# First pair of experts: gate and up weights in units of 512 KB instead of 1 MB

## The chip, the cores and the metric

The kernel runs on one core of a Trainium2 chip. The metric is the device time of one execution in microseconds (us). Before the change three runs took 1047.30, 1050.07 and 1051.92 us, with a median of 1050.07 us. The core's engines are TensorE (PE, with its weight loads PEld), VectorE (DVE), ScalarE (ACT), GpSimd (POOL) and SyncE (SP); transfers run on 16 DMA engines, and nearly all are issued by SP.

## What is computed

The reference is one layer of a decoder: 256 tokens of width 2048, four kinds of attention side by side, an output projection, and then a mixture of experts, which is where the change lies. A router gives each token two of 16 experts, and each expert is a gated network with 512 hidden columns:

```python
for e in range(N_EXPERTS):                                   # 16
    he = jax.nn.silu(t @ w_gate[e]) * (t @ w_up[e])          # (256, 2048) @ (2048, 512)
    y = y + combine[:, e:e + 1] * (he @ w_down[e])           # (256, 512) @ (512, 2048)
```

All is float32. An expert's gate, up and down weights are 4 MB each, so that the 16 experts have 192 MB of weights (MB is 1024 KB throughout). Each is read from memory once.

## The kernel before

**Stages.** The adaLN vectors, the input projection with the attention, and the output projection come first (to about 540 us); then the router, and then eight pairs of experts, `for p in range(NP)` at L1427 ff. (the lines named here are those of the profile). Up to 64 tokens an expert are gathered into slots. A pair's two experts stand side by side on TensorE: expert e = 1 on the upper 64 output partitions (L202), e = 0 on the lower (L205), so that one step is two matmuls of 512 columns.

**One pair.** The contraction of gate and up over 2048 runs in four blocks c of 512, and in each block in four steps i of 128. `GUORDER` sets the order of blocks and of gate (g = 0) and up (g = 1): gate and up of c = 0, gate and up of c = 1, gate of c = 2 and 3, up of c = 2 and 3. Then come silu and product (`sg`, `he`), four transposes (`hpT`), and the down projection `dn` in four blocks n of 512 output columns, each over four steps f of 128. A block's result is scaled (`yo`), split (`yhl`) and scattered back to the tokens by matmuls `sco`, one block later. In the first pair the gather of the tokens (`pg`, `xg`) and the gate vector's spreading (`ada_r`) run between the steps.

**The stream of weights.** `Stream` holds a list of units, in the order in which they are used, and the buffers that are free. Its `pump` takes the next unit, gives it a buffer and issues its transfer on SP; if no buffer fits, it stops, and units behind it wait too. A unit of gate or up is one block c of one expert: 128 partitions x 2048 elements, 1 MB, `(("gu", p), c, g, e)`. A unit of down is 0.5 MB, `(("dh", p, h), f, e)`: step f for half h of the output columns. Buffers are of these kinds:

- five ring buffers `r0` to `r4` of 1 MB, which are given out whole or as two halves; a unit of 1 MB needs both halves of one of them (the method `room`);
- one buffer of 0.5 MB, and several of 1 MB in other pools, which a unit of 1 MB takes whole; two units of 0.5 MB can share one, and it is given on when both are done;
- two of 1 MB that are used once and not given on (`ONCE`).

In the trace a tile takes the name of its unit (`ugu` gate or up, `udh` down, `uo` output projection) or of its ring buffer (`r`). Together they hold 13.5 MB of expert weights when the router runs.

**Order.** A scheduler orders each engine's instructions with its own estimate of times. SP's queue is worked off strictly in order: a transfer whose buffer isn't free yet holds up those behind it. Each transfer also waits for the one issued eight places earlier.

## Time and profile before

| | before |
|---|---|
| median of three runs | 1050.07 us |
| profiled execution | 1046.43 us |
| its span | 1044.7 us |
| TensorE busy | 947.1 us (91%) |
| VectorE busy | 542.3 us (52%) |
| ScalarE busy | 351.0 us (34%) |
| DMA packets moved | 371.12 MB in bytes of 10^6, mean 355 GB/s |

The profiled execution is one run of the program, 3.6 us under the median; its times are counted from the start of the span. A busy TensorE is not one at its peak, since matmuls overlap. The DMA share of a stretch says how much of it the 16 engines were moving data; the GB/s beside it what they moved. In a list of instructions, the time in brackets is the idle time of the engine before the row and what ended it.

### The profile page before, as it was taken

What the parts mean: (1) busy time and instruction counts of PE and PEld (TensorE: products, weight loads), DVE (VectorE), ACT (ScalarE), POOL (GpSimd) and SP (SyncE); (2) the same over time, 40 slices, a digit from 0 to 9 for tenths busy, and PEclk for the clock granted to TensorE, in tenths of its full rate; (3) what the DMA queues carried; (4) which work ended last, traced back from release to release, by engine and by line L of the source; (5) the groups of instructions that cost most, each with busy time, mean ns of one, the idle gap of its engine ahead of it and who ended that gap; (6) DMA issues with size and microseconds to landing.
All of it is one profiled execution on the core that took longest, in us unless ns stands there. A gap on an engine that the chain in (4) does not pass through costs nothing.

```text
span 1044.7 us, 16307 instructions
## 1 busy us (share of the span) xinstructions
PE 947.1 (91%) x6369; PEld 583.4 (56%) x6369; DVE 542.3 (52%) x1058; ACT 351.0 (34%) x759; POOL 4.3 (0%) x13
## 2 busy tenths in 40 slices
PE   5899999999999998789989998999989897999984
PEld 1677778898788986567874434323343232432323
DVE  2444466996998998879764242404033130412216
ACT  4333345566676767634453101100010000200013
POOL 0000000000000000000000000000000000000000
PEclk9999999999999999979989999999999999999997
DMA  9999999996999998799864999999999999999993
GB/s 331 357 356 360 357 326 346 347 371 213 344 329 349 343 384 319 257 331 389 303 237 159 382 419 404 420 415 416 419 412 420 412 420 413 417 417 414 420 375 108
DMA packets 149467, 371.12 MB, mean 355 GB/s; under 512 B 11485, under 2 KB 90246, under 8 KB 132746
## 3 DMA queue, kind: packets, MB, share of 16 engines
q1 hardware_dynamic: 148416, 368.41, 94.5%
q10 hardware_dynamic: 938, 1.61, 0.4%
q8 instruction: 52, 0.85, 0.3%
q14 instruction: 29, 0.24, 0.1%
q0 software_dynamic: 32, 0.01, 0.0%
HBM read 367.90 MB, written 2.10 MB: 354 GB/s over the span
## 4 chain that ended last, share of the span: by engine, by line
PE 66%; DMA 17%; DVE 10%; issue 3%; ACT 3%; SPq 0%; DVEq 0%; ACTq 0%
PE dn L202 11%; DMA r<-in_exp_w_up_dram 8%; PE acc L563 5%; PE acc L564 4%; PE acc L565 4%; PE gatep L202 4%; PE upp L202 4%; PE upp L205 3%; PE pg L1408 3%; PE oacc L567 3%; PE gatep L205 3%; PE oacc L568 3%; PE oacc L569 3%; PE ada L202 2%; DMA r<-in_w_in_dram 2%
## 5 line engine op out<-in xcount | busy, mean ns | idle before, releaser
L563 PE MATMUL acc<-Hh,wlo 128*128 128x256 f32 x512 | 145.0, 293 | 6.0 <-DVE wlo L588 3.6
L564 PE MATMUL acc<-Hl,whi 128*128 128x256 f32 x512 | 145.2, 286 | 0.0
L565 PE MATMUL acc<-Hh,whi 128*128 128x256 f32 x512 | 144.4, 285 | 0.0
L588 DVE TENSOR_TENSOR wlo<-r,whi 128x1024 fp32r<-128x1024 f32 x86 | 104.9, 1220 | 50.1 <-ACT whi L586 49.9
L586 ACT CAST whi<-r 128x1024 fp32r<-128x1024 f32 x86 | 90.0, 1048 | 85.8 <-PE acc L565 23.3
L512 DVE SCALAR_TENSOR_TENSOR ada_v<-r,cT,ada_v 128x1024 f32<-128x1024 f32 x92 | 117.7, 1279 | 0.5
L563 PEld LDWEIGHTS acc<-Hh,wlo 128*128 128x128 f32 x512 | 95.6, 191 | 16.6 <-DVE wlo L588 6.3
L1462 DVE TENSOR_TENSOR he<-upp,sg 128x128 f32<-128x128 f32 x32 | 7.1, 282 | 181.7 <-PE upp L205 181.7
L564 PEld LDWEIGHTS acc<-Hl,whi 128*128 128x128 f32 x512 | 97.8, 191 | 3.5 <-issue 2.6
L565 PEld LDWEIGHTS acc<-Hh,whi 128*128 128x128 f32 x512 | 97.7, 191 | 2.7 <-issue 2.3
L205 PE MATMUL upp<-ugu,xg 128*64 128x512 f32 x196 | 81.7, 597 | 1.3 <-DMA ugu<-in_exp_w_up_dram 1.3
L205 PE MATMUL gatep<-r,xg 128*64 128x512 f32 x192 | 80.4, 596 | 0.0
L205 PE MATMUL upp<-r,xg 128*64 128x512 f32 x172 | 72.6, 595 | 4.0 <-DMA r<-in_exp_w_up_dram 4.0
L1541 ACT CAST yhl<-yo 128x512 fp32r<-128x512 f32 x31 | 19.2, 618 | 167.5 <-DVE yo L1535 142.2
L205 PE MATMUL gatep<-ugu,xg 128*64 128x512 f32 x176 | 72.5, 602 | 0.7 <-DMA ugu<-in_exp_w_gate_dram 0.7
L1492 DVE TENSOR_TENSOR xt<-xt,sco 128x512 f32<-128x512 f32 (+1 forms) x70 | 42.0, 638 | 57.6 <-PE sco L1491 57.0
L205 PE MATMUL dn<-udh,heT 128*64 128x512 f32 x136 | 66.3, 599 | 0.0
L202 PE MATMUL dn<-udh,heT 128*64 128x512 f32 x128 | 63.3, 599 | 1.6 <-DVE heT L1479 1.6
L567 PE MATMUL oacc<-wlo,Oh 128*128 128x512 f32 (+1 forms) x160 | 59.5, 373 | 4.6 <-DVE wlo L588 2.9
L1458 ACT ACTIVATE sg<-gatep 128x512 f32<-128x512 f32 x8 | 4.8, 597 | 169.1 <-PE gatep L205 169.1
L202 PE MATMUL gatep<-ugu,xg 128*64 128x512 f32 x112 | 58.7, 610 | 1.7 <-DMA ugu<-in_exp_w_gate_dram 1.7
L202 PE MATMUL dn<-r,heT 128*64 128x512 f32 (+1 forms) x124 | 59.1, 578 | 0.5 <-DVE heT L1479 0.5
(399 smaller groups left out, 1889.3 us busy)
## 6 DMA issues: line engine op xcount, KB each, us to landing
r<-in_ada_w_dram SPq DMA_DIRECT2D x155, 512.0 KB, 7.2
ugu<-in_exp_w_gate_dram SPq DMA_DIRECT2D x36, 1024.0 KB, 13.3
r<-in_w_in_dram SPq DMA_DIRECT2D x69, 512.0 KB, 7.5
ugu<-in_exp_w_up_dram SPq DMA_DIRECT2D x34, 1024.0 KB, 14.6
udh<-in_exp_w_down_dram SPq DMA_DIRECT2D x66, 512.0 KB, 11.4
r<-in_exp_w_up_dram SPq DMA_DIRECT2D x30, 1024.0 KB, 14.1
r<-in_exp_w_down_dram SPq DMA_DIRECT2D x57, 512.0 KB, 11.4
r<-in_exp_w_gate_dram SPq DMA_DIRECT2D x28, 1024.0 KB, 13.8
```

Source lines behind the costliest of these rows:

```text
L202: ins = op(*args, **kw).ins
L205: ins = op(*args, **kw).ins
L512: V.scalar_tensor_tensor(acc, w, cT[:, u:u + 1], acc[:], OP.mult, OP.add)
L563: ins = mm(o, wl, hh, start=first, stop=False)
L564: mm(o, wh, hl, start=False, stop=False)
L565: mm(o, wh, hh, start=False, stop=last)
L567: ins = mm(o, hh, wl, start=first, stop=False)
L568: mm(o, hl, wh, start=False, stop=False)
L569: mm(o, hh, wh, start=False, stop=last)
L586: A.copy(hi, w)
L588: V.tensor_tensor(lo, w, hi[:].bitcast(F32), OP.subtract)
L1492: V.tensor_tensor(y(t, cs), y(t, cs), o, OP.add)
```

## The change

In the first pair (p = 0) a unit of gate or up is half a block, two of its four steps for one expert: 128 partitions x 1024 elements, 0.5 MB, with a key that has the half h behind it. For each block and each of gate and up there are four transfers in place of two: h = 0 of both experts, then h = 1 of both. Such a unit fits any buffer, a half of a ring buffer too. It is reported done after its two steps, instead of after all four. Units of the other seven pairs, and all down units, stay as they are, and no matmul is added or taken away.

```diff
-        us = [((("gu", p), c, g, e), mkg(c, g, e), 2) for c, g in GUORDER for e in range(2)]
+        def mkg2(c, g, e, h):
+            return lambda t: nc.sync.dma_start(t, (gateT, upT)[g][:, c, 2 * p + e, 1024 * h:1024 * h + 1024])
+
+        if p == 0:
+            us = [((("gu", p), c, g, e, h), mkg2(c, g, e, h)) for c, g in GUORDER for h in range(2) for e in range(2)]
+        else:
+            us = [((("gu", p), c, g, e), mkg(c, g, e), 2) for c, g in GUORDER for e in range(2)]
...
             keys = [(("gu", p), c, g, e) for e in range(2)]
+            half = lambda e, i: (keys[e] + (i // 2,), i % 2) if p == 0 else (keys[e], i)
...
                 for e in (1, 0):
-                    w = stream.get(keys[e])[:, 512 * i:512 * i + 512]
+                    key, at = half(e, i)
+                    w = stream.get(key)[:, 512 * at:512 * at + 512]
...
-            for key in keys:
-                stream.done(key)
+                if p == 0 and i % 2:
+                    for e in range(2):
+                        stream.done(half(e, i)[0])
+            if p:
+                for key in keys:
+                    stream.done(key)
```

The built program shows how the units stand. The number behind a tile's name is that of the buffer's allocation. SP's queue, first place: the transfers behind the last ones that find a free buffer, in pair 0's gate and up. The digits after `ugu` are p, c, g, e, and in the new kernel also h; those after `udh` are p, h, f, e. Before:

```order
L257 DMA ugu0301_6019<-in_exp_w_gate_dram 128x2048
L257 DMA ugu0310_6147<-in_exp_w_up_dram 128x2048
L257 DMA r2_96<-in_exp_w_up_dram 128x2048
L260 DMA r3_97<-in_exp_w_down_dram 128x1024
L260 DMA udh0001_6190<-in_exp_w_down_dram 128x1024 x2
L257 DMA r1_95<-in_exp_w_up_dram 128x2048
```

Now:

```order
L271 DMA ugu03011_6032<-in_exp_w_gate_dram 128x1024
L271 DMA ugu03011_6032<-in_exp_w_up_dram 128x1024
L271 DMA r0_94<-in_exp_w_up_dram 128x1024
L271 DMA r2_96<-in_exp_w_up_dram 128x1024
L271 DMA r4_98<-in_exp_w_up_dram 128x1024
L271 DMA ugu03110_6163<-in_exp_w_up_dram 128x1024
L260 DMA r1_95<-in_exp_w_down_dram 128x1024
L271 DMA r2_96<-in_exp_w_up_dram 128x1024
```

The last up units of c = 2 and 3 go, half by half, to halves of r0, r2 and r4; before, the two of c = 3 took two whole buffers, a 1 MB one and r1.

SP's queue, second place: the transfers that wait for the end of pair 0's gate and up and for its down projection. Before:

```order
L257 DMA r2_96<-in_exp_w_gate_dram 128x2048
L260 DMA udh0131_6335<-in_exp_w_down_dram 128x1024 x2
L260 DMA udh0121_6310<-in_exp_w_down_dram 128x1024 x2
L260 DMA udh0111_6307<-in_exp_w_down_dram 128x1024 x2
L257 DMA r1_95<-in_exp_w_up_dram 128x2048
L257 DMA ugu1001_6360<-in_exp_w_gate_dram 128x2048
L260 DMA udh1001_6507<-in_exp_w_down_dram 128x1024
L257 DMA ugu1011_6397<-in_exp_w_up_dram 128x2048
```

Now:

```order
L260 DMA r0_94<-in_exp_w_down_dram 128x1024
L257 DMA ugu1000_6353<-in_exp_w_gate_dram 128x2048
L260 DMA udh0130_6346<-in_exp_w_down_dram 128x1024 x2
L260 DMA udh0120_6325<-in_exp_w_down_dram 128x1024 x2
L260 DMA udh1000_6523<-in_exp_w_down_dram 128x1024
L257 DMA r2_96<-in_exp_w_gate_dram 128x2048
L257 DMA ugu1010_6412<-in_exp_w_up_dram 128x2048
L257 DMA r1_95<-in_exp_w_up_dram 128x2048
```

Before, the last transfer that waits for gate and up of pair 0 alone is `ugu1001`; now it is the one to r2, a unit of 1 MB earlier, and `ugu1010` waits for the down projection. A half of r0 and one of r4, which held up weights of c = 3, take nothing until units of 1 MB of pair 1 go to r0 and r4, behind the down projection.

TensorE, third place: the middle of pair 0's down projection, behind its first two blocks. Before:

```order
L1386 MATMUL sp_6535<-ident_80,oh4_6074 128x128 x2
L202 MATMUL dn_6417<-r0_94,heT_6373 64x512
L205 MATMUL dn_6417<-r4_98,heT_6373 64x512
L202 MATMUL dn_6417<-udh0111_6307,heT_6373 64x512
L205 MATMUL dn_6417<-r0_94,heT_6373 64x512
```

Now:

```order
L1392 MATMUL sp_6553<-ident_80,oh4_6089 128x128 x2
L202 MATMUL gatep_6489<-r2_96,xg_6100 64x512
L205 MATMUL gatep_6489<-ugu1000_6353,xg_6100 64x512
...
L202 MATMUL dn_6432<-r3_97,heT_6388 64x512
L205 MATMUL dn_6432<-udh0031_6256,heT_6388 64x512
L202 MATMUL dn_6432<-r0_94,heT_6388 64x512
L205 MATMUL dn_6432<-r4_98,heT_6388 64x512
```

Pair 1's gate of c = 0 (eight matmuls) has moved ahead of blocks n = 2 and 3 of the down projection; before, it stands behind both.

## Rows read from the trace of the kernel before

**Rows 1.** The page: span, then DMA share and GB/s in 40 slices

```profile
span 1044.7 us, 16307 instructions
...
DMA  9999999996999998799864999999999999999993
GB/s 331 357 356 360 357 326 346 347 371 213 344 329 349 343 384 319 257 331 389 303 237 159 382 419 404 420 415 416 419 412 420 412 420 413 417 417 414 420 375 108
```

**Rows 2.** Chain of waits in order of time: start us, us, what

```profile
685.66 15.01 DMA r<-in_exp_w_up_dram
...
982.19 16.70 DMA r<-in_exp_w_up_dram
```

**Rows 3.** Windows of 10 us: engines' busy time and count, PEclk, DMA share, GB/s

```profile
540.00:550.00 10.00, 5.79 (x29) 4.90 (x30) 8.21 (x36) 9.87 (x18) 0.00 (x0) 0.60 0.50 198
550.00:560.00 10.00, 10.00 (x48) 4.43 (x46) 5.72 (x12) 5.12 (x9) 0.00 (x0) 0.89 0.00 0
560.00:570.00 10.00, 10.00 (x54) 4.33 (x50) 3.65 (x7) 1.13 (x2) 0.00 (x0) 1.00 0.72 267
570.00:580.00 10.00, 10.00 (x58) 5.21 (x56) 3.22 (x7) 1.49 (x3) 0.00 (x0) 1.00 0.98 374
580.00:590.00 10.00, 10.00 (x50) 3.49 (x46) 1.60 (x6) 2.67 (x4) 0.00 (x0) 1.00 0.90 338
590.00:600.00 10.00, 9.48 (x51) 4.20 (x50) 2.01 (x7) 0.59 (x1) 0.00 (x0) 1.00 1.00 404
600.00:610.00 10.00, 10.00 (x46) 3.27 (x42) 5.41 (x10) 1.85 (x3) 0.00 (x0) 1.00 1.01 419
640.00:650.00 10.00, 7.52 (x48) 4.78 (x44) 3.42 (x9) 2.43 (x5) 0.00 (x0) 1.00 1.04 403
660.00:670.00 10.00, 10.00 (x46) 3.43 (x44) 5.84 (x9) 1.85 (x3) 0.00 (x0) 1.00 1.02 419
```

**Rows 4.** Timeline of SP, its issues: start us, us, engine, line, operation

```profile
541.31 0.33 SPq L257 DMA_DIRECT2D ugu<-in_exp_w_gate_dram  x1
560.57 0.33 SPq L257 DMA_DIRECT2D ugu<-in_exp_w_up_dram  x1
560.99 0.38 SPq L257 DMA_DIRECT2D r<-in_exp_w_up_dram  x1
...
591.89 0.33 SPq L257 DMA_DIRECT2D r<-in_exp_w_up_dram  x1
592.31 0.38 SPq L257 DMA_DIRECT2D ugu<-in_exp_w_gate_dram  x1
```

**Rows 5.** Timeline of TensorE in pair 0 and at pair 1's start

```profile
555.58 0.59 PE L205 MATMUL upp<-r,xg 128*64 128x512 f32 x1
...
559.95 0.59 PE L205 MATMUL upp<-r,xg 128*64 128x512 f32 x1
...
594.18 0.64 PE L202 MATMUL dn<-udh,heT 128*64 128x512 f32 x1 [0.52 <-DVE heT L1479]
...
601.57 0.64 PE L202 MATMUL dn<-r,heT 128*64 128x512 f32 x1
...
605.15 0.72 PE L1490 MATMUL sco<-yhl,M 128*128 128x512 f32 x2
...
606.28 0.64 PE L202 MATMUL dn<-r,heT 128*64 128x512 f32 x1
...
610.18 0.64 PE L202 MATMUL gatep<-ugu,xg 128*64 128x512 f32 x1
...
613.76 0.50 PE L1490 MATMUL sco<-yhl,M 128*128 128x512 f32 x1
```

**Rows 6.** Windows of 2 us, columns as in rows 3

```profile
560.00:562.00 2.00, 2.00 (x14) 1.20 (x12) 0.28 (x1) 0.00 (x0) 0.00 (x0) 1.00 0.33 49
562.00:564.00 2.00, 2.00 (x12) 0.57 (x8) 1.45 (x3) 0.56 (x1) 0.00 (x0) 1.00 0.82 336
```

**Rows 7.** The page, part 6: a group of issues, us to landing

```profile
udh<-in_exp_w_down_dram SPq DMA_DIRECT2D x66, 512.0 KB, 11.4
```

## The prediction

> **What bounds the kernel now.** I read the page's slices first. The 16 DMA engines are busy nine tenths or more from about 575 us to the end, at 404 to 420 GB/s, after a dip at 520 to 575 us [rows 1]. So from there on the kernel runs at the pace of the weight stream. The chain of waits says the same: six times TensorE ends a pair of experts waiting 15 to 20 us for an up weight, first at 685.66 us, last at 982.19 us [rows 2]. What follows the last of these is TensorE's and VectorE's tail. The end therefore moves by as much as the stream moves, and the stream's place is fixed by the last moment at which the queue had nothing to do. In the windows of 10 us that is the dip: 198 GB/s, then 0, then 267, 374, 338, then 404 and 419 [rows 3]. TensorE is busy nearly all of these windows but the first, so it isn't TensorE that waits there. SyncE's own rows tell why the stream stops: between the issues at 541.31 and 560.57 us lie 19 us, and it then goes on with two units of 1 MB [rows 4]. All buffers are full, and the first to come free are those of the up weights of c = 0, when TensorE has read both units whole, at 560.5 us [rows 5]; the gate units of c = 0 sit in the two buffers that are used once and free nothing.
>
> **A ledger of the stream.** I count in MB of 1024 KB; 419 GB/s is 0.40 MB/us. When the stream stops, 13.5 MB of expert weights have landed (13 units of 1 MB and a down unit). With the windows of [rows 3] the kernel before has moved 16.05 MB by 570 us, 19.6 by 580, 22.85 by 590, 26.7 by 600, 30.7 by 610, and so 31.5 MB at 612.0 us. From then on it doesn't stop.
>
> **What the change adds and moves.** Sixteen units of 1 MB become 32 of 0.5 MB: the same bytes, 16 more issues of 0.33 us on SyncE [rows 4], which waits for buffers anyway: nothing. No matmul is added. Eight transfers can be in flight (each also waits for the one eight places ahead), which with halves is 4 MB or 10 us of the stream: it doesn't run dry for that, nothing. Before the stop, one half unit now stands ahead of the last two w_out units, 0.5 MB or 1.25 us; TensorE is busy throughout there, so I take nothing, at worst 1.25 us.
>
> What can bring time is the start. A half comes free when two of the four steps have read it. The first pair of halves (up, c = 0) has been read by 556.1 us [rows 5], 4.4 us before the units were. From the issue at 560.57 to full rate is about 2 us (49 GB/s in 560 to 562, 336 in 562 to 564 [rows 6]), so each transfer starts 2.0 us after its buffer comes free. I went through the new queue in this way, release by release, with TensorE's times of before, since its order in the first pair's gate and up is unchanged and none of its weights comes later. 1 MB moves from 558.1 to 560.6, 1 MB from 562.5 to 565.0, 1 MB from 566.3 to 568.8, and so on. It has moved 17.0 MB by 570, 20.6 by 580, 23.4 by 590 and 26.7 by 600. The lead over before is 1.0, 1.0, 0.55 and 0 MB. It is 2.5 us at best, and it is lost by 600 us, for two reasons that the order shows.
>
> First, halves that can't be used. Units of 1 MB of the later pairs need both halves of one buffer. The last up weights (c = 3, expert 0) now sit in one half of r0 and one of r4, whose other halves hold down weights. They come free by 591.8 us, but the next units are 1 MB; the two halves, 1.0 MB or 2.5 us, lie empty until the third and fourth blocks of the down projection have read the others. So at 591.8 us the new queue has issued up to 26.5 MB, where before it was 27.5 (issues at 591.89 and 592.31 [rows 4]). It runs dry at 597.8 and goes on at 599.6 us: the next buffer comes free with the fourth step of the down projection, 594.18 + 4 x 0.86 = 597.6 us. A step is two matmuls side by side: 0.86 us, from four steps between 601.57 and 605.15 [rows 5].
>
> Second, the order on TensorE. The scheduler now puts pair 1's gate of c = 0 ahead of the down projection's blocks 2 and 3 of pair 0. It takes 3.58 us (610.18 to 613.76 [rows 5]) and delays the release of the down units behind it. The up unit that goes to r3 and starts at 31.5 MB waits for the first step of block 3. That step ends at 601.57 + 3.58 + 1.72 (two steps) + 1.13 (four scatter matmuls, 605.15 to 606.28 [rows 5]) + 1.72 + 0.95 (the step, with its last record) = 610.7 us; its data moves from 612.7 us. The queue has the units to 31.5 MB moved at 612.2 us, stops for half a microsecond, and goes on.
>
> **The sum.** Before, the stream passes 31.5 MB at 612.0 us; now at 612.7 us: +0.7 us. Behind that place the new queue has 6 MB ready (15 us) and doesn't stop again. Both orders end alike: the last up unit ends at 185.5 MB of 192 in both. One of the four broadcasts of the final gain (about 0.6 us each with its copy) moves ahead of the last up weights, from behind them: below 1 us either way, taken as nothing. The profiled execution took 1046.43 us for a span of 1044.7; it becomes 1047.1. It lies 3.6 us under the median of the three runs, 1050.07 us, which becomes 1050.8 us.
>
> **Bounds.** Without the two losses the lead of 1.0 MB stays: -2.5 us, and the earlier start can't give more than 4.4 us. With both losses paid in full, one after the other, and none of the lead it is 2.5 + 3.6 = +6.1 us. I stay near the ledger's end, since its steps are all rows of this stretch.
>
> **What speaks against smaller units.** The trace moves 512 KB units of 4 KB lines (down weights) at almost the rate of the 1 MB units: 403 GB/s in 640 to 650, where they are most of the traffic, against 419 in 660 to 670 [rows 3]. A unit takes 11.4 us from issue to landing [rows 7], nine times its 1.25 us at the stream's rate, so many are in flight together. The Trainium skill's page "DMA: Bandwidth & Descriptors" has, in its section Bandwidth, a rule against this change: batch transfers to 1 MiB or more to get at least 75% of the peak. By its fit in the section on the anatomy of one DMA (2.0 us plus the bytes at 436 GB/s) 32 halves, one after another, would take 32 us longer than 16 units: an estimate from that page alone, 1083 us. The trace doesn't agree, at 403 GB/s for halves in a full queue. What is left of it as a mechanism of this kernel is rival (2).
>
> **The rivals.** (1) The lead stays: if the wait at 597.8 us is not seen, because TensorE runs the down steps earlier, -2.5 us, 1047.6 us. For it speaks that the queue has the lead until 590 us; against it the 0.5 MB pieces that lie empty in the order itself. Chance 0.12.
> (2) Halves move slower. The 512 KB units of the first stages ran at 331 to 360 GB/s [rows 1], with lines of 1 KB (256 columns). At 331 (0.316 MB/us) the new queue reaches 26.5 MB at 601 us instead of 597.8, pair 1's gate waits about 1 us, and 31.5 MB is passed some 2.5 us later than before: 1052.6 us. The 403 GB/s speak against it. Chance 0.06, the page's rule with it.
> (3) Slower, by a look-ahead that is 1 MB shorter in pair 2. There the new queue issues up to 54.5 MB by the time the first two down blocks of pair 1 are read, where before it was 55.5. By the ledger the stream still has about 0.6 MB, 1.5 us, in hand when the next buffer comes free (near 667 us). If TensorE is later than that by more than 1.5 us, the queue stops there for up to 2.5 us, and again after pairs 3 and 5, which have the same gather: up to 7.5 us, 1058 us. The full 419 GB/s there before (660 to 670 us [rows 3]) speaks against a stop. Chance 0.10.
> (4) Something in the new order gains more than the ledger holds, over 5 us: 0.04.
>
> **How the numbers follow.** The forecast, within about 2 us of +0.7, has 0.68. Its time is 1050.8 us. A measurement tells apart about 0.5%, 5.25 us. Rivals (1) and (2) stay within it; (3) goes past it if at least two of its three stops come, 0.08 of its 0.10, and 0.01 of the forecast's case lies at the upper bound of +6.1 us; (4) is the chance of faster. That gives faster 0.04, same 0.87, slower 0.09. The range takes in (1) and (2) and 1.5 us for the spread of medians (the three runs lie at 1047.3 to 1051.92): 1047.6 - 1.5 = 1046.1 to 1052.6 + 1.5 = 1054.1 us.
>
> **What would show it.** In the changed profile the stop should end near 558 us instead of 562, and the windows 560 to 590 should each carry more than 267, 374 and 338 GB/s. Then there should be a short new dip between 597 and 600 us, and perhaps one near 612, where there was none. The first long wait for an up weight should come within 1 us or so of 685.66. I am wrong if the stream has no dip after 595 us and the long waits come 2 us or more earlier, or if the windows from 655 to 670 us show a stop.

## The result: slower by half a per cent

The changed kernel took 1056.47 us, the median of seven runs (1053.55 to 1059.18); the kernel before 1051.92 us in the same comparison. The ratio is 1.0051, with a 95% interval of 1.0028 to 1.0074: 5.4 us slower. Timed again beside the experiments it was 1.0057 (1.0037 to 1.0076). The forecast was 1050.8 us, with a range of 1046.1 to 1054.1 us, and "no difference" as by far the likeliest. That was wrong: the change costs about 5 to 6 us, and by the intervals 3 to 8 us.

### The profile page after: what moved, and what is told of

Read it like the earlier page. It is cut to its first block, busy times and chain, and to the rows that moved or that the text cites. A ratio compares the mean times of both kernels' runs of the same rounds, so it can differ in the third digit from the quotient of the medians.

```text
span 1053.0 us, 16336 instructions
## 1 busy us (share of the span) xinstructions
PE 952.7 (90%) x6369; PEld 587.8 (56%) x6369; DVE 541.8 (51%) x1058; ACT 351.0 (33%) x759; POOL 4.3 (0%) x13
## 4 chain that ended last, share of the span: by engine, by line
PE 63%; DMA 19%; DVE 10%; issue 4%; ACT 3%; SPq 0%; DVEq 0%; ACTq 0%
PE dn L202 9%; DMA r<-in_exp_w_up_dram 5%; PE acc L569 5%; PE upp L202 4%; PE gatep L202 4%; PE acc L570 4%; PE acc L571 4%; PE pg L1414 3%; PE upp L205 3%; DMA ugu<-in_exp_w_gate_dram 3%; DMA r<-in_ada_w_dram 3%; PE gatep L205 3%; DMA r<-in_exp_w_gate_dram 3%; PE oacc L573 2%; DMA r<-in_w_in_dram 2%
## 5 line engine op out<-in xcount | busy, mean ns | idle before, releaser
L205 PE MATMUL upp<-r,xg 128*64 128x512 f32 x184 | 78.4, 598 | 0.0
L205 PE MATMUL upp<-ugu,xg 128*64 128x512 f32 x184 | 77.7, 603 | 0.0
L205 PE MATMUL gatep<-ugu,xg 128*64 128x512 f32 x192 | 77.7, 618 | 0.0
L205 PE MATMUL gatep<-r,xg 128*64 128x512 f32 x176 | 77.6, 632 | 0.0
L202 PE MATMUL gatep<-ugu,xg 128*64 128x512 f32 x104 | 57.8, 645 | 11.1 <-DMA ugu<-in_exp_w_gate_dram 11.1
L202 PE MATMUL dn<-r,heT 128*64 128x512 f32 (+1 forms) x130 | 56.9, 558 | 1.6 <-DVE heT L1491 1.6
```

What stands on the lines that cost most here:

```text
L202: ins = op(*args, **kw).ins
L205: ins = op(*args, **kw).ins
```

## The profile after

The profiled execution took 1054.75 us. The page's second part (span, TensorE's granted clock, DMA share and GB/s in 40 slices) answers [rows 1]:

```profile
span 1053.0 us, 16336 instructions
...
PEclk6999999999999999879989999999999999999987
DMA  9999999996999998799946999999999999999992
GB/s 331 357 357 359 357 327 323 346 365 221 335 336 349 353 383 312 244 335 386 357 161 209 363 405 406 409 406 417 418 412 418 404 421 413 416 417 415 419 353 83
```

The span is 8.3 us longer than before, but not all of that is the change's. The first slice already runs at a lower clock. The place from which the change can act is the first step of pair 0's gate. TensorE's timelines of before, of the changed kernel, and of the kernel before with two unused matmuls in its last pair (an experiment below) have this row for it:

```profile
551.47 0.99 PE L202 MATMUL gatep<-ugu,xg 128*64 128x512 f32 x1
```

```profile
553.98 0.64 PE L202 MATMUL gatep<-ugu,xg 128*64 128x512 f32 x1
```

```profile
555.80 0.77 PE L202 MATMUL gatep<-ugu,xg 128*64 128x512 f32 x1
```

The third kernel has the same program as before up to the last pair and yet is 4.3 us later there, so this place moves from run to run. From it to the end of the span the third kernel takes 1049.0 - 555.8 = 493.2 us, and before 1044.7 - 551.5 = 493.2 us, the same to a tenth. So I count all times from here on from the first gate step. Nothing of the change's cost is lost from sight by that: over all profiles of this document the first gate step lies at 551.5 to 559.5 us (mean 556.0) in the six profiles with whole units in pair 0, and at 552.4 to 560.0 us (mean 555.8) in the eight profiles with halves there. The landmark itself is good to some 0.2 us, since the clock was still at its lower level for its first step in some profiles (0.99 us against 0.64). The changed kernel takes 1053.0 - 554.0 = 499.0 us: 5.8 us more.

**The stream.** Windows from the first gate step on, of before and then of the changed kernel (columns as in [rows 3]):

```profile
551.47:569.97 18.50, 18.50 (x91) 7.52 (x90) 7.90 (x15) 4.78 (x9) 0.00 (x0) 0.98 0.39 144
569.97:579.97 10.00, 10.00 (x58) 5.18 (x56) 3.22 (x7) 1.46 (x3) 0.00 (x0) 1.00 0.97 372
579.97:589.97 10.00, 10.00 (x50) 3.52 (x46) 1.60 (x6) 2.70 (x4) 0.00 (x0) 1.00 0.90 340
589.97:599.97 10.00, 9.48 (x52) 4.20 (x50) 1.98 (x7) 0.59 (x1) 0.00 (x0) 1.00 1.00 403
599.97:609.97 10.00, 10.00 (x47) 3.24 (x41) 5.42 (x9) 1.85 (x3) 0.00 (x0) 1.00 1.02 420
609.97:619.97 10.00, 10.00 (x46) 3.83 (x48) 3.67 (x8) 0.62 (x1) 0.00 (x0) 1.00 1.01 419
...
669.97:679.97 10.00, 10.00 (x48) 3.91 (x44) 4.14 (x8) 0.62 (x1) 0.00 (x0) 1.00 1.01 420
```

```profile
553.98:572.48 18.50, 18.50 (x91) 7.34 (x90) 8.18 (x15) 5.03 (x10) 0.00 (x0) 1.00 0.58 193
572.48:582.48 10.00, 10.00 (x56) 5.22 (x56) 3.21 (x7) 1.66 (x3) 0.00 (x0) 1.00 0.96 332
582.48:592.48 10.00, 10.00 (x48) 3.48 (x44) 1.59 (x6) 2.50 (x4) 0.00 (x0) 1.00 0.95 348
592.48:602.48 10.00, 9.48 (x50) 4.20 (x50) 2.18 (x7) 0.59 (x1) 0.00 (x0) 1.00 0.96 349
602.48:612.48 10.00, 9.51 (x44) 3.59 (x42) 3.87 (x7) 1.24 (x2) 0.00 (x0) 1.00 1.00 392
612.48:622.48 10.00, 10.00 (x47) 4.16 (x44) 4.99 (x10) 1.24 (x2) 0.00 (x0) 1.00 1.00 400
...
672.48:682.48 10.00, 10.00 (x46) 3.45 (x44) 4.01 (x8) 0.62 (x1) 0.00 (x0) 1.00 0.98 397
```

The gain of the early start is in the first line: 49 GB/s more over 18.5 us, 0.86 MB. It goes in the next ones: 372 against 332, 403 against 349, 420 against 392, 419 against 400. Summed, the changed kernel is 0.02 MB ahead 48.5 us behind the first gate step and 0.42 MB behind at 68.5 us. Farther on it loses a little more, as in the last line of each (397 against 420); at 448.5 us, just before the last weights, it is 1.04 MB behind, which is 2.6 us of the stream at 0.40 MB/us.

**The tail.** TensorE's timeline in the last pair (the time in brackets is the idle time before the row), of before and then of the changed kernel: the first step of the last gate block, the broadcasts `pf` of the final gain, the first step of the down projection:

```profile
993.96 0.64 PE L202 MATMUL gatep<-ugu,xg 128*64 128x512 f32 x1 [1.36 <-DMA ugu<-in_exp_w_gate_dram]
...
1003.28 1.12 PE L1472 MATMUL pf<-fa,ident 4*128 4x512 f32 x2 [0.69 <-ACT udn L1473]
...
1010.76 0.64 PE L202 MATMUL dn<-r,heT 128*64 128x512 f32 x1
```

```profile
998.96 1.12 PE L202 MATMUL gatep<-ugu,xg 128*64 128x512 f32 x1 [3.82 <-DMA ugu<-in_exp_w_gate_dram]
...
1008.56 1.12 PE L1484 MATMUL pf<-fa,ident 4*128 4x512 f32 x2
1010.36 1.44 PE L1484 MATMUL pf<-fa,ident 4*128 4x512 f32 x2 [0.68 <-ACT r L1485]
...
1018.86 0.64 PE L202 MATMUL dn<-r,heT 128*64 128x512 f32 x1 [0.52 <-DVE heT L1491]
```

From the first gate step the last gate block's weights come after 993.96 - 551.47 = 442.5 us before and after 998.96 - 553.98 = 445.0 us now: 2.5 us later, the stream's lag. TensorE waits 3.82 us for them instead of 1.36. And then the tail is longer: 19.9 us from there to the first down step, where it was 16.8. The windows (granted clock: third number from the end) say why:

```profile
998.00:1004.00 6.00, 5.04 (x12) 1.46 (x14) 0.00 (x0) 0.00 (x0) 0.00 (x0) 0.50 1.01 414
...
1011.00:1014.00 3.00, 3.00 (x8) 0.77 (x8) 0.00 (x0) 0.58 (x1) 0.00 (x0) 0.50 1.04 396
```

TensorE stood still for 3.82 us, and its clock was then granted at 0.50 (1.2 GHz) until about 1004 us, so that a matmul of the gate block takes 1.12 us instead of 0.64. It comes out late, does two broadcasts ahead of the last up block where it did one, with a wait of 0.68 us for ScalarE between them, and runs part of the last up block at 0.50 again (1011 to 1014). What follows is as long as before: 1053.0 - 1018.86 = 34.1 us against 33.9. So of 5.8 us, 2.5 are the stream's, 3.1 the tail's, and 0.2 the end's.

Two long pieces of the chain show how far the lag comes through; they answer the two of [rows 2]:

```profile
689.54 15.30 DMA r<-in_exp_w_up_dram
...
980.13 18.79 DMA ugu<-in_exp_w_gate_dram
```

Such a piece is a transfer's time from its issue to its landing. The prediction took the six of them for waits of TensorE of 15 to 20 us. They are not: before, TensorE stands still for 1.3 to 1.4 us at the end of each, and for 16 us in all from the first gate step on while weights are on their way. So TensorE has little slack beside the stream. Counted from the first gate step, the first of the two transfers is issued at 135.6 us (before 134.2) and lands at 150.9 (before 149.2), 1.7 us later; the last one is now for a gate unit.

## The experiments

All times are beside the kernel before on the same chip. The table has, for each kernel, the ratio to before with its interval; the time from the first gate step to the end of the span in its profile (before 493.2 us); and how many MB all its transfers have moved at 48.5, 68.5, 118.5 and 448.5 us behind the first gate step, less what before has moved by then. These I counted from the packets in the traces. The kernel before with unused matmuls is within 0.12 MB of before throughout, so smaller differences mean nothing; the four profiles with the changed queue lie up to some 0.5 MB apart at one place.

| kernel | ratio (95%) | us | 48.5 | 68.5 | 118.5 | 448.5 |
|---|---|---|---|---|---|---|
| changed | 1.0051 (1.0028 to 1.0074) | 499.0 | +0.02 | -0.42 | -0.45 | -1.04 |
| changed, again | 1.0057 (1.0037 to 1.0076) | 496.6 | -0.29 | -0.93 | -0.98 | -1.24 |
| broadcast back | 1.0046 (1.0029 to 1.0063) | 496.2 | -0.05 | -0.78 | -0.68 | -1.39 |
| changed, wait filled | 1.0043 (1.0028 to 1.0059) | 495.8 | -0.03 | -0.68 | -0.52 | -0.84 |
| before, wait filled | 1.0004 (0.9987 to 1.0021) | 493.2 | +0.04 | +0.05 | +0.09 | +0.12 |
| gate behind | 1.0048 (1.0026 to 1.0069) | 501.1 | -0.10 | -0.62 | -0.62 | -1.33 |
| split only | 1.0011 (0.9993 to 1.0028) | 493.7 | +0.06 | +0.06 | -0.06 | -0.09 |
| halves in pairs 0, 1 | 1.0048 (1.0026 to 1.0070) | 499.5 | +0.27 | +0.06 | -0.79 | -0.98 |
| halves in all pairs | 1.0025 (1.0007 to 1.0043) | 497.0 | +0.30 | +0.09 | -0.09 | -2.39 |
| halves in pair 1 | 1.0044 (1.0018 to 1.0071) | 498.4 | -0.06 | -0.60 | -0.83 | -1.25 |
| last blocks whole | 1.0018 (0.9995 to 1.0041) | 496.8 | +0.31 | -0.68 | -0.57 | -1.42 |
| halves in the last pair | 0.9960 (0.9938 to 0.9981) | 491.5 | -0.04 | -0.04 | -0.12 | -0.48 |
| halves in its last up blocks | 0.9989 (0.9969 to 1.0008) | 493.4 | +0.08 | +0.08 | +0.07 | +0.03 |

### The tail

**The changed kernel again.**

> The changed kernel as it is, a second time. Theory (tail): of the 5 us that the change costs, about 2.4 us come from a stream that is 0.95 MB behind in the last pair, and about 3 us from the tail, because TensorE waits 3.8 us instead of 1.4 us before the last gate block, its clock falls to half, and one broadcast of the final gain then stands ahead of the last up block just when its weights land. Then this profile too shows about 0.9 to 1.0 MB behind and a granted clock of 0.5 near the last gate block (some 5 us of it), and the ratio is again about 1.005. Rival (chance): the lower clock in the first profile's tail was an accident of that run; then the tail here takes 6.9 us from the landing of the last up unit to the first down step, as in the kernel before, not 9.9, and the ratio is nearer to 1.002.

The ratio came again. TensorE's rows at the same places, and the window behind the wait:

```profile
1003.24 1.11 PE L202 MATMUL gatep<-ugu,xg 128*64 128x512 f32 x1 [3.83 <-DMA ugu<-in_exp_w_gate_dram]
...
1020.55 0.64 PE L202 MATMUL dn<-r,heT 128*64 128x512 f32 x1 [0.52 <-DVE heT L1491]
```

```profile
1003.00:1007.00 4.00, 3.76 (x10) 1.14 (x12) 0.00 (x0) 0.00 (x0) 0.00 (x0) 0.57 1.01 416
```

The wait is the same 3.83 us and the clock falls again, but it is back at 1.00 by 1007 us, and the tail loses only 17.3 - 16.8 = 0.5 us. The stream is 1.24 MB behind, more than in the first profile. So the theory holds for the stream, and for the clock in kind; the tail's size was that of the first run only.

The two profiles are of one program, so the broadcast stands equally early in both. What differs is how long the clock was at 0.50 between the wait and the first down step: 10.2 us in the first profile, 3.4 us here. So at least 2.6 of the first profile's 3.1 us are the clock's, and the broadcast's place is worth 0.5 us at most. The other profiles fit. From the last gate block to the first down step it takes 16.3 to 16.8 us in the six with whole units in the last pair in which the clock stays at 1.00, 17.3 and 19.0 where it was at 0.50 for 3.4 us (here and halves in pair 1), 19.9 for 10.2 us (the first profile and halves in pairs 0 and 1), and 21.4 for 13.6 us (gate behind).

**One broadcast put back.** In the changed kernel the scheduler has put the third broadcast ahead of the last up block; here it waits for that block, as before.

```diff
+            ulast = bt.prev
...
-                    mm(pf[:], ident[0:4, q:q + 1].broadcast_to([4, 128]), fa8[:], start=True, stop=True)
+                    pfm = mm(pf[:], ident[0:4, q:q + 1].broadcast_to([4, 128]), fa8[:], start=True, stop=True).ins
+                    if q == 2:
+                        behind(pfm, ulast)
```

Here `behind` tells the scheduler to put one instruction behind another, and `bt.prev` is the last matmul of a block.

> The changed kernel with one broadcast of the final gain put behind the last up block again, where it stands in the kernel before; nothing else moves. If the moved broadcast is what the tail loses by, the last up block starts with the landing of its weights and the time falls by about 2.5 us against the changed kernel (ratio to before about 1.0025). If the tail loses by the clock alone, the half clock stays at the last gate block and the gain is below 1 us. If neither is the cause (only the stream is late), no change.

```profile
1000.89 0.64 PE L202 MATMUL gatep<-ugu,xg 128*64 128x512 f32 x1 [3.91 <-DMA ugu<-in_exp_w_gate_dram]
```

```profile
1001.00:1005.00 4.00, 3.55 (x16) 0.95 (x16) 0.00 (x0) 0.38 (x1) 0.00 (x0) 1.00 1.00 412
```

The ratio is 1.0046, about 1 us better than the changed kernel beside it and within the intervals. The tail takes 16.5 us from the gate block to the first down step, as before. But in this run the clock stayed at 1.00 though TensorE had stood still for 3.91 us. So the broadcast and the clock can't be told apart by this profile. By the ratios both together are worth about 1 us in the mean, not 3, and the intervals don't tell that 1 us from nothing.

**The wait filled.** Four matmuls of 128 x 512 that nobody reads, on data that is there, ahead of the last gate block; in the kernel before two of them.

```diff
+            if p == NP - 1 and n in (5,):
+                wm = ps("PT", [128, 512], name="wm")
+                bt.prev = glast
+                for j in range(4):
+                    bt(mm, wm[:], ident, g2r[:, 512 * j:512 * j + 512], start=j == 0, stop=j == 4 - 1)
...
+            glast = bt.prev
```

> The changed kernel with four matmuls of 128x512 that nobody reads, placed in TensorE's wait before the last pair's last gate block (3.8 us); the scheduler then also puts the broadcast back behind the last up block. Theory (tail): the granted clock stays at 1.0 to the end, landing of the last up unit to first down step takes 6.9 us instead of 9.9, and the time falls by 3 us to about 1.0023 of before: what is left is the stream's 2.4 us. Rival: the clock at the gate block is hidden by the wait for the last up unit; then this run equals the one with the broadcast put back. Rival (stream only): no change against the changed kernel.

```profile
996.43 3.70 PE L205 MATMUL wm<-g2r,ident 128*128 128x512 f32 x8
1000.33 0.64 PE L205 MATMUL gatep<-ugu,xg 128*64 128x512 f32 x1 [0.20 <-DMA ugu<-in_exp_w_gate_dram]
```

> The kernel before with two such matmuls in the same wait, which is 1.4 us there. In the one profile of before the clock stays at 1.0 in the tail, so by the theory nothing is to be gained: ratio 1.000 within 0.001 (two matmuls of 0.85 us may overrun the wait by 0.3 us, which the later wait takes up). If the kernel before also loses its clock there in many of its runs, the ratio is below 0.999.

With the wait filled the clock stays, and the tail takes 16.5 us. The scheduler has also put the broadcast back behind the last up block here, so this run, too, tests both together. The ratio is 1.0043, against 1.0057 of the unchanged one beside it: 1.5 us, again not 3, and again within the intervals. In the kernel before the same trick gives nothing (1.0004), as expected. So the best estimate of the tail is 1 to 1.5 us of the 5 to 6 in the mean, though it was 3.1 us in the first profile; the ratios alone don't show that it is more than nothing. The rest, 4 us or more, is to be looked for in the stream.

### The stream

**Pair 1's gate put behind the down projection.**

```diff
+                if p == 1 and n == 0 and i == 0:
+                    bt.prev = dnlast
...
+                dnlast = bt.prev
```

> The changed kernel with pair 1's gate of c = 0 put behind the last two blocks of pair 0's down projection again, as in the kernel before; the halves stay. The prediction's second loss (0.7 us from that gate ahead of the blocks, from 0 MB at 600 us to -0.28 MB at 612) should vanish: the stream comes out of 620 us 0.3 MB better than in the changed kernel, 0.7 us. Rival: the moved gate reads two whole units and frees two whole buffers early, which the stream needs more than the halves of the down units; then the stream is 0.3 to 0.5 MB worse at 620 us and the kernel 1 us slower than the changed one. A third: neither, the loss is in the transfers; no change.

The third case came nearest: 0.62 MB behind at 68.5 us, in the middle of what the four profiles with the changed queue show (0.42 to 0.93). The 0.3 MB that either theory looked for would hardly show beside that spread. The way there is another one, though: most of the loss now comes earlier, 0.55 MB from 48.5 to 58.5 us, at a DMA share of 0.94 and 362 GB/s (before 1.02 and 420). So on balance putting the gate back gains nothing that can be seen. The tail was at its worst in this run, 21.4 us from the gate block to the first down step:

```profile
1002.11 1.11 PE L202 MATMUL gatep<-ugu,xg 128*64 128x512 f32 x1 [4.03 <-DMA ugu<-in_exp_w_gate_dram]
...
1023.53 0.64 PE L202 MATMUL dn<-r,heT 128*64 128x512 f32 x1 [0.52 <-DVE heT L1493]
```

**Transfers in halves, buffers whole.**

```diff
+        def mkg2(c, g, e):
+            def load(t):
+                for h in range(2):
+                    nc.sync.dma_start(t[:, 1024 * h:1024 * h + 1024],
+                                      (gateT, upT)[g][:, c, 2 * p + e, 1024 * h:1024 * h + 1024])
+            return load
...
+        us = [((("gu", p), c, g, e), (mkg if p else mkg2)(c, g, e), 2) for c, g in GUORDER for e in range(2)]
```

> The kernel before, with its buffers and whole units, but in pair 0 each unit of gate and up is fetched by two transfers of 512 KB into the two halves of its 1 MB buffer. It has the change's transfers without its buffers. If smaller transfers cost nothing (theory: buffers and order cost the time), the ratio to before is 1.000 within 0.001 and the stream is level with before at 620 us. If halves move slower or their queue is too shallow, the loss between 570 and 620 us comes here too: 0.3 to 0.6 MB, 1 to 1.5 us.

The stream is level with before at every place, to 0.1 MB, and the ratio is 1.0011 with 1 in its interval. So it isn't the size of pair 0's transfers. What is left of the change is which buffers the units take, when these come free, and the order that follows from it.

**Halves in pairs 0 and 1, and in all pairs.** Here and below the change's condition `p == 0` becomes another one, where the units are listed and where they are read: first `p < 2`, then `True`.

```diff
-        if p == 0:
-            us = [((("gu", p), c, g, e, h), mkg2(c, g, e, h)) for c, g in GUORDER for h in range(2) for e in range(2)]
-        else:
-            us = [((("gu", p), c, g, e), mkg(c, g, e), 2) for c, g in GUORDER for e in range(2)]
+        us = []
+        for c, g in GUORDER:
+            if p < 2:
+                us += [((("gu", p), c, g, e, h), mkg2(c, g, e, h)) for h in range(2) for e in range(2)]
+            else:
+                us += [((("gu", p), c, g, e), mkg(c, g, e), 2) for e in range(2)]
```

> Halves for gate and up of pairs 0 and 1, whole units from pair 2 on. Theory: what loses is the border where units that need both halves of a ring buffer follow units that filled it half by half. Here the border lies one pair later, so the lead of 0.9 MB that the early start gives at 560 to 570 us should stay at about 0.5 MB to 650 us, and be lost at the end of pair 1 (about 655 to 665 us), to some 0.8 MB behind. Rival (halves move slower): no lead at 620 to 650 us either, and more loss, since there are twice as many halves.

Windows of halves in pairs 0 and 1 (columns as above), at the place where the changed kernel loses and at the end of pair 1, and of before at the latter:

```profile
590.90:600.90 10.00, 9.36 (x48) 4.08 (x48) 1.64 (x6) 0.59 (x1) 0.00 (x0) 1.00 1.00 393
600.90:610.90 10.00, 10.00 (x46) 3.37 (x42) 3.96 (x7) 1.31 (x3) 0.00 (x0) 1.00 1.03 408
...
650.90:660.90 10.00, 9.30 (x56) 5.79 (x57) 2.90 (x6) 2.26 (x4) 0.00 (x0) 0.99 0.90 341
```

```profile
649.97:659.97 10.00, 9.13 (x53) 5.15 (x54) 2.38 (x5) 2.00 (x4) 0.00 (x0) 1.00 1.01 405
```

At 48.5 us the stream is still 0.27 MB ahead and at 68.5 us level, where the changed kernel is 0.4 to 0.9 MB behind. The loss comes one pair later, in the last window: 341 GB/s where before had 405. The place is as the theory of the border has it, but the lead of 0.5 MB that was to stay until then did not: it was 0.27 MB at 48.5 us and 0.06 at 68.5, as the rival had it. In this order, pair 1's halves go to just those halves of `r0` and `r4` that lie empty in the changed kernel.

> Halves for gate and up of all eight pairs, so that there is no border. Theory: the lead of about 0.5 MB (1.2 us) stays to the end, and the last up weights also come in halves, so that the last step waits for half as much: 2 to 5 us faster than before (ratio 0.995 to 0.998). Rival (halves move slower, 4 KB lines and half the bytes in flight): the stream falls behind by a few tenths of a MB in every pair, and the kernel is slower than the changed one.

Without a border there is no such window. But the stream falls behind all the same, slowly: 2.39 MB at the end, 6 us. The last window of 150 us, of before and of this kernel:

```profile
849.97:999.97 150.00, 134.53 (x592) 48.79 (x594) 32.03 (x62) 11.15 (x19) 0.00 (x0) 0.99 1.02 416
```

```profile
853.37:1003.37 150.00, 129.97 (x574) 46.56 (x576) 31.36 (x60) 11.15 (x19) 0.00 (x0) 0.99 1.03 409
```

A full queue of halves moves 409 GB/s, one of mixed units 416: 1.7% less at the same busy share. It isn't the fewer bytes in flight that makes this difference: counted packet by packet in the kernel before, from 118.5 to 448.5 us, the 4 KB packets of the down units take 163 ns in the mean and the 8 KB packets of gate and up 315 ns, which is 402 and 416 GB/s over 16 engines, and in this kernel the 4 KB packets take 163 ns as well. My theory (a lead that stays, 2 to 5 us faster) fell; the rival was right on the rate, though not on the time: this kernel (1.0025) is not slower than the changed one. In its order the last up unit ends at 184.0 MB of the queue's 192, where before and the changed kernel have it at 185.5; the 1.5 MB are 3.7 us of the stream. That would leave 2.3 of the 6 us, near the ratio's 2.6; it is worked out, not tested.

**Two tests of the border.** Halves in pair 1 alone, and the change without the last two up blocks of pair 0:

```diff
+            if p == 1:
```

```diff
+            if p == 0 and (c, g) not in ((2, 1), (3, 1)):
```

> Halves for gate and up of pair 1 alone; pair 0 and the others have whole units. The border from halves to whole units lies at the end of pair 1, where the run with halves in pairs 0 and 1 lost 0.69 MB between 650 and 660 us. Theory: the border itself costs, wherever it lies; then this run is level with before to 650 us and 0.5 to 0.7 MB behind at 660 us, 1.3 to 1.8 us. Rival: at a border the stream only gives back what it had gained, since there the buffers and TensorE set how far it may be ahead; with no early start there is nothing to give back, and it stays within 0.2 MB of before.

Both theory and rival missed the place. At the end of pair 1 nothing is lost, 408 GB/s where before has 405:

```profile
654.93:664.93 10.00, 9.22 (x58) 6.43 (x59) 3.47 (x7) 2.83 (x5) 0.00 (x0) 0.98 1.02 408
```

The loss comes earlier, 0.54 MB of it between 48.5 and 68.5 us, where pair 0's whole units are followed by halves. So a border from whole units to halves can cost as much as one the other way, and an early start isn't needed for it. And the engines were not idle in that stretch:

```profile
614.93:624.93 10.00, 10.00 (x46) 3.51 (x44) 3.47 (x6) 0.62 (x1) 0.00 (x0) 1.00 1.03 383
```

The share is 1.03, at 383 GB/s where before had 419.

> The change, but the last two up blocks of pair 0 (c = 2 and 3) in whole units, so that no half of a ring buffer with up weights of c = 3 is left alone. The early start at 558 us shrinks: up to 14 MB as before. If the stranded halves are the loss (the prediction's first reason), the stream is level with before or better from 590 us on. Rival: the border only moves into pair 0; by the order, the unit at 29.5 MB now goes to r3 and waits for the first step of the down projection's third block, with 7.25 MB ahead of what TensorE has read, where before it was 8.5 at least; then the stream stops near 608 us and is 0.5 to 1.0 MB behind at 620 us.

The rival's case: +0.31 MB at 48.5 us, -0.68 at 68.5. In this order no half of `r0` or `r4` is left empty behind up weights, and the loss is as large. So a loss needs no halves left empty. By its ratio, 1.0018 with 1 in the interval, this kernel's time isn't told from before's, though the stream in its profile, the slowest of its ten runs, is 1.42 MB behind at 448.5 us.

**A count that fits.** From the built programs I counted, for each transfer, by how many MB SP's queue is ahead of what TensorE must have read when the transfer's buffer comes free. The lowest value between 26 and 34 MB of the expert weights (about 595 to 620 us), beside the change in MB from 48.5 to 68.5 us: before 8.5, and by definition 0; split only 8.5, 0.00; halves in pairs 0 and 1 8.25, -0.21; in all pairs 8.25, -0.21; in pair 1 7.75, -0.54; gate behind 7.25, -0.52; last blocks whole 7.25, -0.99; changed 7.25, -0.44 to -0.73 in its four profiles. Halves in pairs 0 and 1 have their lowest value, 8.0, at 49.5 MB, and that is where they lose (-0.85 MB from 68.5 to 118.5 us); halves in all pairs have 10.0 there at least, and lose 0.18. (The changed kernel also has an 8.0, at 54.5 MB, and loses little by it, being late already.) So in these orders the stream loses where the look-ahead falls below that of before in the stretch in which TensorE is busy nearly all the time. That is a pattern found after the runs, not a cause that was tested: no order was made with halves in pair 0 and a look-ahead of 8.5. It doesn't set the size either, since three orders with 7.25 lose 0.44 to 0.99 MB, and it doesn't say why halves in pair 1 moved 383 GB/s with busy engines.

### A use for the halves

The cost of halves is paid where TensorE is busy and the stream's buffers are scarce. In the last pair it is TensorE that waits, and no whole unit of gate or up follows. So I moved the change to the other end, first for the whole last pair and then for its last two up blocks alone:

```diff
+            if p == NP - 1:
```

```diff
+            if p == NP - 1 and (c, g) in ((2, 1), (3, 1)):
```

> The kernel before with the change's halves in the last pair alone (p = 7); pair 0 has whole units. Theory: halves cost where units of 1 MB follow them and where TensorE doesn't wait for the stream; behind the last pair no whole unit follows, and there TensorE waits for every weight. In the queue's order the last up unit then ends at 184.0 MB of 192 instead of 185.5, which is 3.7 us of stream; 16 MB of halves cost some 0.3 MB, 0.7 us, by the rate at which the stream falls behind with halves in all pairs. Expected: 2 to 4 us faster than before, ratio 0.996 to 0.998, and the last step's first down matmul starts 5 to 7 us behind the last up weights. Rival: the tail is bound by TensorE (its matmuls of the last pair stand in a row from 999 us on) and not by those weights; then the ratio is 0.999 to 1.001. Second rival: the smaller pieces make TensorE wait longer before a gate block and its clock falls; then 1.000 or above.

> The kernel before with halves only for the last pair's up units of c = 2 and 3 (4 MB). The last up unit ends at 184.5 MB instead of 185.5. Theory: half of the gain of the run with the whole last pair in halves, at less cost in rate: 1 to 3 us faster than before, ratio 0.997 to 0.999. Rivals as there.

Halves in the last pair are faster than both kernels, as expected: ratio 0.9960 (0.9938 to 0.9981), 2 to 6.5 us, median 1048.45 us against 1051.18. The profile shows less, 491.5 us from the first gate step to the end against 493.2; it is of the slowest of the twelve runs. Its first down step, with the first gate step of the same timeline:

```profile
559.46 1.12 PE L202 MATMUL gatep<-ugu,xg 128*64 128x512 f32 x1
...
1015.71 0.64 PE L202 MATMUL dn<-r,heT 128*64 128x512 f32 x1 [0.52 <-DVE heT L1494]
```

That is 456.3 us behind the first gate step, 3.0 less than before (1010.76 - 551.47 = 459.3). From there to the end it takes 35.2 us where before took 33.9, so 1.3 us are given back. With only the last two up blocks in halves the ratio is 0.9989, and 1 is in its interval: not told from no change.

## Why the prediction was wrong, step by step

**Right: when things come free.** The prediction put the first pair of halves at 556.1 us, the next free buffer at 597.6 us and the wait of the unit for `r3` at 610.7 us. SP's rows of the changed kernel answer [rows 4]:

```profile
558.50 0.80 SPq L271 DMA_DIRECT2D r<-in_exp_w_up_dram  x2
...
600.19 0.33 SPq L257 DMA_DIRECT2D ugu<-in_exp_w_up_dram  x1
...
613.69 0.33 SPq L257 DMA_DIRECT2D r<-in_exp_w_up_dram  x1
```

Less the 2.5 us by which the first gate step is later, these are 556.0, 597.7 and 611.2 us. The two short dips came as well. By the forecast they lie, 2.5 us later, at 600.3 to 602.1 and near 615 us:

```profile
601.00:602.00 1.00, 1.00 (x7) 0.29 (x4) 0.06 (x1) 0.00 (x0) 0.00 (x0) 1.00 0.96 270
...
615.00:616.00 1.00, 1.00 (x6) 0.29 (x4) 0.06 (x1) 0.00 (x0) 0.00 (x0) 1.00 0.81 287
```

The lead at the start was right too: 0.86 MB (forecast 1.0), and nothing left 48.5 us on (forecast 0 at 600 us).

**Mis-sized: the stream at 612 us.** The sum had it 0.28 MB behind there (0.7 us). Measured at 68.5 us, 620 us by before's time, are 0.42, 0.93, 0.78 and 0.68 MB in the four profiles with the changed queue: 0.7 MB in the mean, 1.75 us. The step that failed is the assumption in the ledger that a queue that isn't empty moves 0.40 MB/us. In the windows between 48.5 and 68.5 us the DMA share is 0.99 to 1.00 and the only stop is the short one at 615 us, but they carry 392 and 400 GB/s, in the second run 382 and 390, where before has 420 and 419. The transfers' rows of the page's kind for 599 to 616 us show a thinner queue: a median of 6.8 us from issue to landing for the up units to the ring, where the kernel before had 8.9 in 596.5 to 613.5:

```profile
r<-in_exp_w_up_dram SPq DMA_DIRECT2D x4, 1024.0 KB, 6.8
```

```profile
r<-in_exp_w_up_dram SPq DMA_DIRECT2D x2, 1024.0 KB, 8.9
```

Counted from SP's issues and their landings, 2.3 MB were in flight in the mean between 48.5 and 58.5 us, where before had 3.7 (the landings of one in eight transfers can't be followed, so both are an eighth too low). So the slower stretch has the thinner queue. That the one makes the other isn't shown: with halves in pair 1 a window was slower still, 383 GB/s, at a share of 1.03.

**Seen, but not the difference: the second loss.** Pair 1's gate ahead of the down blocks was to cost 0.7 us. Its wait and its dip are there, at 613.69 and 615 us. But with the gate put back the stream stops at another place and is as late (-0.62 MB). And of the first loss the reason was too narrow: halves left empty may be one way to lose look-ahead, but an order without them lost as much.

**Half right: rival (3).** I gave a shorter look-ahead in pair 2 a chance of 0.10 and a price of up to 7.5 us. It comes: the window at 672 to 682 us has 397 GB/s where before has 420, with a short stop in it, and the stream goes from -0.45 MB at 118.5 us to -1.04 at 448.5. In the second run it is -0.98 to -1.24.

```profile
674.00:675.00 1.00, 1.00 (x8) 0.28 (x4) 0.00 (x0) 0.00 (x0) 0.00 (x0) 1.00 0.76 254
```

So 0.3 to 0.6 MB, 0.7 to 1.5 us: more than the sum's 0 ("doesn't stop again"), far less than the rival's price. The rival's condition was a TensorE more than 1.5 us late there, and the four profiles with the changed queue bear it out. In pair 1's down projection, about 110 us behind the first gate step, TensorE is 2.3, 2.9, 2.7 and, with the wait filled, 1.4 us later than before; from 118.5 to 168.5 us the stream loses 0.4, 0.2, 0.4 and 0.0 MB. Why the loss doesn't add up from pair to pair isn't shown; that a late stream meets buffers that are already free would be one reason.

**Not seen: the tail.** "Both orders end alike" was the wrong step here; the broadcast that moves, "taken as nothing: below 1 us either way", was priced rightly, at 0.5 us or less. The sum has no term for TensorE's clock, and a lag of the stream isn't passed on one for one. It makes TensorE's wait before the last gate block 2.5 us longer, and then the clock may fall. In the profiles the tail cost 3.1, 0.5, 4.6 (gate behind) and, with the broadcast back or the wait filled, 0 us; by the ratios with the broadcast back or the wait filled it is 1 to 1.5 us in the mean, not told from nothing. The Trainium skill's page "TensorE: Matmul & The Clock Gate" describes this in its section "HAM oscillation — how this bites in real kernels": a wait for a DMA that brings the next slice of an operand lets the clock fall, and the next piece of work starts slow. The trace agrees in the changed kernel's two profiles (0.50 and 0.57 behind waits of 3.82 and 3.83 us) and not in the one with the broadcast back (1.00 behind 3.91 us).

**The sum, as measured.** Stream 1.04 to 1.24 MB, 2.6 to 3.1 us, and tail 0.5 to 3.1 us make the 3.4 and 5.8 us of the two profiles. The ratios say 5.4 and 6.0 us, with intervals of 2 us to either side. The two profiles have 4.6 us in the mean and the ratios 5.7; the 1 us between them isn't accounted for and lies within those intervals.

**Rival (2), the smaller transfers,** was rightly low. The rule of the page "DMA: Bandwidth & Descriptors" (Trainium skill, section Bandwidth: batch to 1 MiB or more) stands there beside measurements of transfers issued from GpSimd, and the page's fit that the prediction used is for that path, too; the weights here are issued by SP. The trace shows little of it: 409 against 416 GB/s where all gate and up weights come in halves. For the change itself it costs nothing that can be measured: the split transfers ran at 1.0011 (0.9993 to 1.0028).

The rest of what should have shown it: the first window did carry more (193 against 144), the next one did not (332 against 372), the third a little (348 against 340), and the transfer taken for the first long wait was issued 1.4 us late, not within 1 us. The windows from 655 to 670 us show no stop; the one at 674 us lies behind them.

## What to carry to other kernels

Where TensorE is the bound for a while and the buffers are full, an earlier start of the stream can be a loan only: here a lead of 0.86 MB was gone after 48.5 us. Count the lowest point of the queue's look-ahead in that stretch before and after: an edit of the units' size moves it in ways that only the whole order shows. In these runs smaller pieces paid at the end of the stream, where the consumer waits for the last bytes, and not at its start. And don't carry a lag to the end one for one: look at which wait it lengthens, and at what TensorE's clock does behind that wait.

## What the runs showed of the hardware

A DMA share of 1.00 is no full rate: 382 to 400 GB/s stood beside shares of 0.99 to 1.00, and 383 beside 1.03, where other windows had 419 and 420 at 1.01 and 1.02. A stream in which all gate and up weights come as 4 KB lines moves 409 GB/s, one with 8 KB lines for them 416; a 4 KB packet takes 163 ns in both, an 8 KB one 315. Equal waits of TensorE did not have equal results: behind 3.82, 3.83 and 3.91 us the clock was at 0.50 for about 6 us, at 0.57 over 4 us, and at 1.00. And the time at 0.50 is what the work behind such a wait pays for: 16.5 us without it, 17.3 with 3.4 us of it, 19.9 with 10.2.
